# A two-layer attention and retention trunk: the second layer's value projections in couples, and its last output projections joined in one tail

## The chip, the cores and the metric

The kernel runs on one core of a Trainium2 chip. The metric is the device time of one execution in microseconds. The engines are TensorE (PE in the profile; PEld is its weight load), VectorE (DVE), ScalarE (ACT), GpSimd (POOL) and SyncE (SP, which here issues DMAs). L316 and the like are lines of the kernel.

## The reference

512 tokens of width 1024 pass two layers, and a last RMS norm closes them. Layer 0 mixes with causal forgetting attention (12 heads of 128), layer 1 with retention (12 heads, keys of 64, values of 128); both also have 4 heads of cross-attention to 256 memory rows. Each layer is

```python
h = rmsnorm(x, norm_g[i])
q, k, v, ..., q_mem, z = split_cols(h @ w_in, sizes)
o = concat([main(q, k, v), memo(q_mem)], axis=-1) * silu(z)
x = x + o @ w_out[i]
```

In layer 1, `main` is retention: rotary q and k, scores times a decay table, their product with v, and an RMS norm per head. The output is `rmsnorm(x, final_norm_g)`.

## The kernel before

**Split products.** Every matrix product is made of three matmuls on 32-bit parts: a value is cast to a high part H by ScalarE, VectorE subtracts it from the value to make a low part L, and the product is HH + HL + LH. A weight piece of 128x1024 therefore costs a load (raw), an ACT cast (wH, L130) and a DVE subtraction (wL, L131). There are 4 buffers for each of wH and wL and 3 for raw; a piece is prepared when an older one is retired (`retire`, `prep_piece`).

**Layout.** The tokens are 4 blocks of 128 rows. The normed activations h stand transposed as hH and hL. q, k, the memory queries and the gates z are projected feature-major (`f_T`, L209: 24 matmuls of 512 columns in two parts; `f_z` is the gate, `f_rot` adds the rotary step). Heads are worked in pairs: pair p has heads 2p and 2p+1.

**Rotation.** `f_rot` copies the accumulator out (ACT, L243), sends it through four DMAs that swap 32-row groups (SP, L246), multiplies by sine and cosine and adds (DVE, L248 to L250), and splits the sum into the qk tiles (ACT and DVE, L254 to L262; for k the last step is L256). The scores of the pair (`g_ret`, L610) read the qk tiles.

**Values.** `f_v` (L266) makes the values of one pair: 24 matmuls with 256 moving columns for each token block, from two weight pieces. `f_v2` (L299) makes those of two neighbouring pairs: 24 matmuls of 512 columns per block in two parts of 12, from four pieces; it yields eight parts, two per block. Layer 1 uses `f_v` for pairs 0 and 5 and `f_v2` for (1,2) and (3,4).

**Output.** `f_out` multiplies finished gated heads by the output weights for one pair or for two pairs at a time, and adds to x (L336). `f_out_last` makes the very last output projection: it opens three accumulators with the terms that do not need the last gated head, lets that head finish, and closes them.

**Order.** The program is a list of cycles. Each cycle has fillers (parts of projections, in a list) and jobs (steps of the attention or retention generators), and `emit` places a job step after the filler at which it is due; steps not yet due are carried into the next cycle. Tensor matmuls run in exactly this written order. DVE, ACT and POOL are ordered by a scheduler that goes by due times, so the order of their instructions changes when the lists change, but it is fixed in the program. The first cycle of a layer is called its lead, and norm steps of layer 1 (L186 to L196, four token blocks) are carried into the lead. The cycles of layer 1 after the memory heads are numbered by pair, 0 to 5; cycle p computes pair p's heads while its fillers make q and k (`nq`) of pair p+1, the gates `z0` and `z1` of pair p, values, and an output projection.

**End.** `after1` is called on each finished output block of the last layer and makes the final norm: sum of squares (ACT, L813), scale (POOL, L814 and L819), product with the norm weights (DVE, L816), scaling (L821 to L824) and the output DMAs.

Of the kernel before, what the change touches and what calls it, by code (L numbers as in the profile page):

```python
# [36 lines left out]
def tile_hybrid(ctx, tc, x_in, mem_in, memT_in, g_cols, norm_g, fin_g, b_f, wv0, wp, index, consts, cosT, sinT, dec, out):  # L37
# [320 lines left out]
    def f_out_last(l, pr, after, fine=False):  # L358
        keys = [(l, "o", pr, hf) for hf in range(2)]
# [3 lines left out]
        heads = (pr * 2, pr * 2 + 1)  # L363
        opened = {}

        def terms(t, c0, c1):
            o = c0 // 512
            return out_terms(l, pieces[keys[o]], heads, t, c0 - o * 512, c1 - o * 512)

        def begin(blk):  # L370
            ps = acc_tile()[:, :blk[2] - blk[1]]
            for i, (a, b) in enumerate(terms(*blk)[:3]):
                PE.matmul(ps, lhsT=a, rhs=b, start=(i == 0), stop=False)  # L373
            opened[blk] = ps

        def finish(blk):
            ps = opened.pop(blk)
            for i, (a, b) in enumerate(terms(*blk)[3:]):
                PE.matmul(ps, lhsT=a, rhs=b, start=False, stop=(i == 2))  # L379
# [3 lines left out]
        def fn(t):  # L383
            if t == 0:
                for b in blocks[:3]:
# [213 lines left out]
    def g_ret(l, h):  # L599
# [52 lines left out]
        st[l, "g", h] = split_new("gg", sz)  # L652
# [100 lines left out]
    def build_layer(l):  # L753
        M = "fox" if l == 0 else "ret"
# [4 lines left out]
        cycle(f_v(l, 0) + qm[0] + qm[1], start=("lead", l))  # L759
# [5 lines left out]
        v2 = {pr: f_v2(l, (pr, pr + 1)) for pr in (1, 3)}  # L765
        for pr in range(6):
            f = v2[pr][4:] if pr in v2 else []
            z0, z1 = f_z(l, pr * 2), f_z(l, pr * 2 + 1)
            nq = fq(pr + 1) if pr < 5 else []
            if pr == 0:  # L770
                f = f + z0 + z1 + nq[:-2] + f_out(l, (6, 7)) + nq[-2:] + v2[1][:4]
            elif pr in (2, 4):
                o = f_out(l, (pr - 2, pr - 1))
                if pr == 2:
                    f = f + z0 + z1 + nq[:-2] + o + nq[-2:] + v2[3][:4]
                else:
                    f = f + z0 + z1 + nq[:4] + o[:4] + nq[4:] + o[4:]
            elif pr == 5:
                f = f_v(l, 5) + z0 + z1 + f_out(l, (4,))
            elif l == 0:  # L780
                f = f + z0 + z1 + nq
            else:
                f = f + nq + z0 + z1
# [15 lines left out]
    cycle(f_out_last(0, 5, lambda *a: None), [("norm", (t, ("g", 1)), t + 0.5) for t in range(NT)],  # L799
# [5 lines left out]
    def after1(t, c0, c1):  # L805
        src = xt[t][:, c0:c1]
# [3 lines left out]
        ss = small.tile([P, 1], F32, name="ss")  # L810
        r = small.tile([P, 1], F32, name="rstdf", bufs=6)
        junk = tile_("dd", [P, 512])
        A.activation(junk[:, :c1 - c0], src, AF.Square, accum_out=ss)  # L813
        G.tensor_scalar(out=r, in0=ss, scalar1=1.0 / D, scalar2=fin.get((t, "r"), EPS), op0=ALU.mult, op1=ALU.add)  # L814
        fin[t, "r"] = r
        V.tensor_tensor(out=y[:, c0:c1], in0=src, in1=st["g", 2][:, c0:c1], op=ALU.mult)  # L816
        if c1 == D:
            r2 = small.tile([P, 1], F32, name="rstd2")
            G.tensor_tensor(out=r2, in0=r, in1=nhalf, op=ALU.pow)  # L819
            if t >= 1:  # L820
                V.tensor_scalar(out=y[:, :512], in0=y[:, :512], scalar1=r2, scalar2=None, op0=ALU.mult)  # L821
            else:
                A.activation(y[:, :512], y[:, :512], AF.Copy, scale=r2)
            A.activation(y[:, 512:], y[:, 512:], AF.Copy, scale=r2)  # L824
            nc.sync.dma_start(out=out[t * P:(t + 1) * P, :512], in_=y[:, :512])
            A.dma_start(out=out[t * P:(t + 1) * P, 512:], in_=y[:, 512:])

    cycle(f_out_last(1, 5, after1, fine=False), start="end")
# [8 lines left out]
    def emit():  # L837
# [14 lines left out]
        for ci, (fillers, jobs, start, mode, last) in enumerate(cycles):  # L852
# [9 lines left out]
            elif start == "end":  # L862
                st["g", 2] = load_g(fin_g)
            elif start == ("lead", 1):
# [138 lines left out]
```

## Time and profile before

| what | value |
|---|---|
| median of 3 runs | 932.09 us (931.97 to 932.2) |
| the profiled execution | 931.98 us, of it 930.2 us span |
| busy, share of the span | PE 98%, PEld 84%, DVE 64%, ACT 47%, POOL 4% |
| mean granted clock of TensorE | 0.996 |
| mean DMA rate | 108 GB/s |

The span runs from the first to the last recorded instruction; 1.78 us of the time lie outside it. A busy share is a mean over stages. PE is over 90% busy in 38 of the 40 equal slices of the span, all but the first and the last.

### The profile page before, as it was taken

To read this page: it belongs to the slowest core of one execution; us is meant where nothing else is said; L and a number is where in the kernel's file an instruction comes from. 1 tells how busy PE (TensorE), PEld (TensorE's weight loads), DVE (VectorE), ACT (ScalarE), POOL (GpSimd) and SP (SyncE) were. 2 spreads that over 40 slices of the span, in tenths; PEclk is the share of its full clock that TensorE was granted. 3 is DMA by queue.
4 is the path that set the end of the run, shared out by engine and by line. 5 is a ranking of instruction groups with operands and counts; after the bars stand their busy time and mean duration, and the time that the engine had idled before them with its cause. 6 is when DMAs were issued, how large, how long until landed. Compare 5 with 4: busy or idle time off the path is not lost.

```text
span 930.2 us, 12316 instructions
## 1 busy us (share of the span) xinstructions
PE 915.7 (98%) x4611; PEld 777.1 (84%) x4611; DVE 598.3 (64%) x1067; ACT 441.7 (47%) x773; POOL 34.4 (4%) x92
## 2 busy tenths in 40 slices
PE   8999999999999999999999999999999999999995
PEld 6988888888888888888898898888888888888984
DVE  5766664553655564646557756566769676878776
ACT  6654443422544233433325434544557554766464
POOL 0200100000000000000000010000000000000002
PEclk9999999999999999999999999999999999999998
DMA  8963332222322231423232152323324331532302
GB/s 299 337 212 110 111 110 81 90 80 68 125 90 92 72 99 51 139 83 102 80 99 94 46 159 77 105 75 100 98 99 127 93 103 55 159 103 79 115 23 91
DMA packets 32483, 100.69 MB, mean 108 GB/s; under 512 B 4380, under 2 KB 4636, under 8 KB 32424
## 3 DMA queue, kind: packets, MB, share of 16 engines
q1 hardware_dynamic: 30840, 96.76, 32.1%
q0 software_dynamic: 864, 2.10, 0.8%
q10 hardware_dynamic: 720, 1.05, 0.3%
q8 instruction: 36, 0.59, 0.3%
q14 instruction: 23, 0.19, 0.1%
HBM read 92.53 MB, written 4.22 MB: 104 GB/s over the span
## 4 chain that ended last, share of the span: by engine, by line
PE 93%; ACT 2%; DMA 1%; DVE 1%; POOL 1%; issue 1%; POOLq 0%; SPq 0%; ACTq 0%; DVEq 0%
PE acc L220 45%; PE acc L60 21%; PE acc L316 9%; PE s L60 6%; PE o L538 5%; PE acc L434 1%; PE pt L572 1%; PE o L60 1%; DMA x<-in_x_dram 1%; PE pt L507 1%; PE acc L379 1%; PE acc L373 1%; PE pt L196 1%; ACT dd L813 0%; ACT wH L130 0%
## 5 line engine op out<-in xcount | busy, mean ns | idle before, releaser
L131 DVE TENSOR_TENSOR wL<-raw,wH 128x1024 fp32r<-128x1024 f32 x148 | 180.8, 1224 | 99.1 <-ACT wH L130 61.6
L130 ACT CAST wH<-raw 128x1024 fp32r<-128x1024 f32 x148 | 154.6, 1049 | 64.0 <-PE acc L220 31.6
L220 PE MATMUL acc<-hL,wH 128*128 128x512 f32 x608 | 163.5, 395 | 0.0
L220 PE MATMUL acc<-hH,wH 128*128 128x512 f32 x608 | 153.5, 395 | 0.0
L220 PE MATMUL acc<-hH,wL 128*128 128x512 f32 x608 | 150.6, 390 | 0.0
L60 PE MATMUL acc<-wH,gg 128*128 128x512 f32 x448 | 146.6, 393 | 0.0
L220 PEld LDWEIGHTS acc<-hH,wL 128*128 128x128 f32 x608 | 114.2, 188 | 24.4
L220 PEld LDWEIGHTS acc<-hH,wH 128*128 128x128 f32 x608 | 111.2, 188 | 21.2
L220 PEld LDWEIGHTS acc<-hL,wH 128*128 128x128 f32 x608 | 111.2, 188 | 20.6
L60 PEld LDWEIGHTS acc<-wH,gg 128*128 128x128 f32 x448 | 84.2, 188 | 16.8
L60 PE MATMUL acc<-wL,gg 128*128 128x512 f32 x224 | 87.4, 390 | 0.0
L336 DVE TENSOR_TENSOR x<-acc,x 128x512 f32<-128x512 f32 x80 | 54.7, 687 | 36.5 <-PE acc L60 34.5
L151 ACT CAST pTH<-pt 128x128 fp32r<-128x128 f32 (+2 forms) x64 | 29.7, 467 | 63.3 <-PE pt L572 50.6
L562 ACT ACTIVATE p<-dd,nm 128x128 f32<-128x128 f32 (+3 forms) x48 | 27.0, 563 | 67.1 <-DVE nm L558 66.9
L60 PE MATMUL s<-qk 128*128 128x256 f32 (+3 forms) x240 | 53.7, 326 | 0.0
L151 ACT CAST gg<-sz 128x512 fp32r<-128x512 f32 x32 | 19.9, 621 | 64.8 <-DVE sz L473 39.9
L316 PE MATMUL acc<-wH,hH 128*128 128x512 f32 x128 | 50.4, 394 | 0.0
L316 PE MATMUL acc<-wH,hL 128*128 128x512 f32 x128 | 50.0, 390 | 0.0
L316 PE MATMUL acc<-wL,hH 128*128 128x512 f32 x128 | 49.9, 390 | 0.0
L152 DVE TENSOR_TENSOR pTL<-pt,pTH 128x128 fp32r<-128x128 f32 (+2 forms) x64 | 34.3, 537 | 24.3 <-ACT pTH L151 24.1
L60 PEld LDWEIGHTS acc<-wL,gg 128*128 128x128 f32 x224 | 42.2, 188 | 7.7
L538 PE MATMUL o<-pTH,vv 128*128 128x512 f32 (+1 forms) x192 | 48.4, 315 | 0.0
(165 smaller groups left out, 1329.3 us busy)
## 6 DMA issues: line engine op xcount, KB each, us to landing
raw<-in_wp_dram SPq DMA_DIRECT2D x146, 512.0 KB, 3.6
cbc<-c_d SPq DMA_DIRECT2D x12, 256.0 KB, 3.2
cbc<-in_dec_dram SPq DMA_DIRECT2D x12, 256.0 KB, 3.3
dd<-dd SPq DMA_DIRECT2D x48, 64.0 KB, 2.0
x<-in_x_dram SPq DMA_DIRECT2D x4, 512.0 KB, 8.0
raw<-in_wv_dram SPq DMA_DIRECT2D x2, 536.0 KB, 4.2
vv<-in_memT_dram SPq DMA_DIRECT2D x2, 512.0 KB, 4.5
vv<-in_mem_dram SPq DMA_DIRECT2D x2, 512.0 KB, 7.7
```

The lines of the kernel that those rows point to most:

```text
L60: PE.matmul(ps, lhsT=l, rhs=r, start=(i == 0), stop=(i == n - 1))
L130: A.copy(out=H[:, :n], in_=raw[:, :n])
L131: V.tensor_tensor(out=L[:, :n], in0=raw[:, :n], in1=H[:, :n].bitcast(F32), op=ALU.subtract)
L151: A.copy(out=dH, in_=src)
L152: V.tensor_tensor(out=dL, in0=src, in1=dH.bitcast(F32), op=ALU.subtract)
L196: PE.transpose(pt[:, k, :], xn[:, c:c + P], ident)
L220: PE.matmul(box["ps"], lhsT=a[:, k * P:(k + 1) * P], rhs=b[:, k, :], start=(n == 0), stop=(n == 23))
L316: PE.matmul(ps, lhsT=a, rhs=b, start=(k == 0 and n == 0), stop=(k == KD - 1 and n == 2))
L336: V.tensor_tensor(out=dst, in0=ps, in1=dst, op=ALU.add)
L373: PE.matmul(ps, lhsT=a, rhs=b, start=(i == 0), stop=False)
L538: PE.matmul(o[:, j * P:], lhsT=a, rhs=b, start=(j == 0 and i == 0), stop=(j == NT - 1 and i == 2))
L562: A.activation(p[:, :n], dd[:, :n], AF.Exp, bias=nm, scale=-1.0, accum_out=sm)
```

## The change

All value projections of layer 1 are made by `f_v2`, for (0,1), (2,3) and (4,5); the first stands in the lead, the halves of the others at the ends of cycles 1 and 3 and the starts of cycles 2 and 4. The lists of the cycles of layer 1 are rearranged; the output projection of pairs 2 and 3 moves from cycle 4 to cycle 5, between the two gates. The output projections of pairs 4 and 5 are joined in `f_out_last`, which now opens three accumulators with 9 matmuls each instead of 3, and makes the last block in two pieces of 256 columns. The gated heads of pairs 4 and 5 stand in buffers of other tags. The final norm is written in a new way: whole rows are scaled by one DVE instruction, the last block's sum of squares is made on DVE, and DVE, ACT and POOL keep the written order there. Layer 0 keeps its order.

```diff
-    def f_out_last(l, pr, after, fine=False):
-        keys = [(l, "o", pr, hf) for hf in range(2)]
+    def f_out_last(l, prs, after, fine=False):
+        keys = [(l, "o", pr, hf) for hf in range(2) for pr in prs]
         blocks = [(t, c, c + 512) for t in range(NT) for c in (0, 512)]
         if fine:
             blocks[-1:] = [(NT - 1, 512, 768), (NT - 1, 768, 1024)]
-        heads = (pr * 2, pr * 2 + 1)
         opened = {}
+        early = 6 * len(prs) - 3
...
-            return out_terms(l, pieces[keys[o]], heads, t, c0 - o * 512, c1 - o * 512)
+            return sum([out_terms(l, pieces[l, "o", pr, o], (pr * 2, pr * 2 + 1), t, c0 - o * 512, c1 - o * 512) for pr in prs], [])
...
-            for i, (a, b) in enumerate(terms(*blk)[:3]):
+            for i, (a, b) in enumerate(terms(*blk)[:early]):
...
-                for b in blocks[:3]:
+                for b in ((blocks[0], blocks[2], blocks[1]) if len(prs) > 1 else blocks[:3]):
...
-        st[l, "g", h] = split_new("gg", sz)
+        st[l, "g", h] = split_new({4: "km", 5: "qk"}.get(pr, "gg"), sz)
...
-        cycle(f_v(l, 0) + qm[0] + qm[1], start=("lead", l))
+        v2 = {pr: f_v2(l, (pr, pr + 1)) for pr in ((1, 3) if l == 0 else (0, 2, 4))}
+        cycle((f_v(l, 0) if l == 0 else v2[0]) + qm[0] + qm[1], start=("lead", l))
...
-        v2 = {pr: f_v2(l, (pr, pr + 1)) for pr in (1, 3)}
         for pr in range(6):
-            f = v2[pr][4:] if pr in v2 else []
             z0, z1 = f_z(l, pr * 2), f_z(l, pr * 2 + 1)
             nq = fq(pr + 1) if pr < 5 else []
-            if pr == 0:
-                f = f + z0 + z1 + nq[:-2] + f_out(l, (6, 7)) + nq[-2:] + v2[1][:4]
-            elif pr in (2, 4):
-                o = f_out(l, (pr - 2, pr - 1))
-                if pr == 2:
-                    f = f + z0 + z1 + nq[:-2] + o + nq[-2:] + v2[3][:4]
+            o = f_out(l, {0: (6, 7), 2: (0, 1), 4: (2, 3)}[pr]) if pr in (0, 2, 4) else []
+            if l == 0:
+                if pr == 4:
+                    f = z0 + z1 + nq[:4] + o[:4] + nq[4:] + o[4:]
+                elif pr == 5:
+                    f = f_v(l, 5) + z0 + z1 + f_out(l, (4,))
                 else:
-                    f = f + z0 + z1 + nq[:4] + o[:4] + nq[4:] + o[4:]
-            elif pr == 5:
-                f = f_v(l, 5) + z0 + z1 + f_out(l, (4,))
-            elif l == 0:
-                f = f + z0 + z1 + nq
+                    f = (v2[pr][4:] if pr else []) + z0 + z1 + nq if pr % 2 else z0 + z1 + nq[:-2] + o + nq[-2:] + v2[pr + 1][:4]
+            elif pr == 0:
+                f = z0 + z1 + nq + o
+            elif pr in (1, 3):
+                f = nq + z0 + z1 + v2[pr + 1][:4]
+            elif pr == 2:
+                f = v2[2][4:] + z0 + z1 + nq + o
+            elif pr == 4:
+                f, late = v2[4][4:] + z0 + z1 + nq, o
             else:
-                f = f + nq + z0 + z1
+                f = z0 + late + z1
...
+        if last and c0 > 0:
+            r = one("rstdf")
+            prev = fin[t, "r"]
+            V.tensor_tensor_reduce(out=junk, in0=src, in1=src, scale=1.0 / D, scalar=prev, op0=ALU.mult, op1=ALU.add, accum_out=r)
+            fin[t, "r"] = r
+            if c1 < D:
+                return
+            r2 = one("rstd2")
+            G.tensor_tensor(out=r2, in0=r, in1=nhalf, op=ALU.pow)
+            for c in (512, 768):
+                V.scalar_tensor_tensor(out=y[:, c:c + 256], in0=xt[t][:, c:c + 256], scalar=r2, in1=g[:, c:c + 256],
+                                       op0=ALU.mult, op1=ALU.mult)
+                nc.sync.dma_start(out=out[rows, c:c + 256], in_=y[:, c:c + 256])
+            A.activation(y[:, :512], y[:, :512], AF.Copy, scale=r2)
+            A.dma_start(out=out[rows, :512], in_=y[:, :512])
+            return
+        ss = one("ss")
+        A.activation(junk, src, AF.Square, scale=1.0 / 32, accum_out=ss)
+        if "pend" in fin:
+            fin.pop("pend")()
+        r = one("rstdf")
+        G.tensor_tensor(out=r, in0=ss, in1=fin[t, "r"] if c0 else eps_t, op=ALU.add)
+        if last:
+            V.tensor_tensor(out=y[:, :512], in0=src, in1=g[:, :512], op=ALU.mult)
+        if c0 == 0:
+            return
+        r2 = one("rstd2")
+        G.tensor_tensor(out=r2, in0=r, in1=nhalf, op=ALU.pow)
+
+        def scale():
+            V.scalar_tensor_tensor(out=y, in0=xt[t], scalar=r2, in1=g, op0=ALU.mult, op1=ALU.mult)
+            nc.sync.dma_start(out=out[rows, :], in_=y)
+        fin["pend"] = scale
+
+    cycle(f_out_last(1, (4, 5), after1, fine=True), start="end")
...
+                end.enter_context(tc.manual_schedule(engines={mybir.EngineType.DVE, mybir.EngineType.Pool, mybir.EngineType.Activation}))
...
-                ev.append([nF + 1.2, flush_retired])
+                ev.append([nF + 0.2, flush_retired])
```

The first place is the seam of cycles 4 and 5 on PE. `acc_7870` (after) is the key projection of pair 5, `o_7883` the product of head 9 with its values, `acc_7938` the gate of head 10, and `s_7955` the first score of head 10, which reads the rotated keys `qk_7912`. After:

```order
L220 MATMUL acc_7870<-hL_87,wH_7666 128x512 x4
L220 MATMUL acc_7870<-hH_86,wL_7667 128x512 x8
L538 MATMUL o_7883<-pTH_7752,vv_7458 128x256
L538 MATMUL o_7883<-pTL_7753,vv_7458 128x256
L538 MATMUL o_7883<-pTH_7752,vv_7459 128x256
L538 MATMUL o_7883<-pTH_7752,vv_7458 128x128
L538 MATMUL o_7883<-pTL_7753,vv_7458 128x128
L538 MATMUL o_7883<-pTH_7752,vv_7459 128x128
L220 MATMUL acc_7938<-hH_86,wH_7717 128x512 x8
L220 MATMUL acc_7938<-hL_87,wH_7717 128x512 x4
L60 MATMUL s_7955<-qk_7852,qk_7912 128x512
L60 MATMUL s_7955<-qk_7854,qk_7912 128x512
```

Before, the same key projection is `acc_7782`, its rotated keys are `qk_7831`, and what comes behind it is:

```order
L220 MATMUL acc_7782<-hL_87,wH_7588 128x512 x4
L220 MATMUL acc_7782<-hH_86,wL_7589 128x512 x8
L60 MATMUL acc_7843<-wH_7647,gg_7083 128x512
L60 MATMUL acc_7843<-wL_7648,gg_7083 128x512
L60 MATMUL acc_7843<-wH_7647,gg_7084 128x512
L60 MATMUL acc_7843<-wH_7647,gg_7348 128x512
L60 MATMUL acc_7843<-wL_7648,gg_7348 128x512
L60 MATMUL acc_7843<-wH_7647,gg_7349 128x512
L60 MATMUL acc_7843<-wH_7703,gg_7562 128x512
L60 MATMUL acc_7843<-wL_7704,gg_7562 128x512
L60 MATMUL acc_7843<-wH_7703,gg_7563 128x512
```

Before, seven more blocks of that output projection, the steps of heads 8 and 9 and the first value part of pair 5 follow, and only then the score `s_8077<-qk_7757,qk_7831`. After, 6 products with the values and 12 matmuls of a gate stand between the key projection and the score.

The second place is DVE at the same seam, after. `wL_7919` is a weight piece's low part, `dd_7842` the rotation of q of pair 5, `dd_7902` that of k, `km_5068` and `km_5066` are the sine and cosine tables, `km_7820` a part of gated head 8:

```order
L152 TENSOR_TENSOR km_7820<-sz_7714,km_7819 128x512
L248 TENSOR_TENSOR dd_7843<-dd_7843,km_5068 128x512
L249 TENSOR_TENSOR dd_7842<-dd_7842,km_5066 128x512
L131 TENSOR_TENSOR wL_7919<-raw_7721,wH_7918 128x1024
L250 TENSOR_TENSOR dd_7842<-dd_7842,dd_7843 128x512
L633 TENSOR_TENSOR p_7930<-p_7930,dd_7932 64x512
L261 TENSOR_TENSOR qk_7854<-dd_7842,qk_7852 64x512
L648 SCALAR_TENSOR_TENSOR sz_7780<-o_7883,sz_7780 128x512
L635 TENSOR_TENSOR sqs_7931<-p_7930,sqs_7931 64x512
L261 TENSOR_TENSOR qk_7860<-dd_7842,qk_7858 64x512
L248 TENSOR_TENSOR dd_7903<-dd_7903,km_5068 128x512
L249 TENSOR_TENSOR dd_7902<-dd_7902,km_5066 128x512
L250 TENSOR_TENSOR dd_7902<-dd_7902,dd_7903 128x512
L256 TENSOR_TENSOR qk_7912<-dd_7902,qk_7912 64x512
```

The rotation of k (`dd_7902`, `dd_7903`) stands behind the last steps of the rotation of q, behind the weight piece, and behind steps of heads 8 and 9 (`sz_7714`, `p_7930`, `sz_7780`).

The third place is the lead of layer 1 on DVE. `hL` are low parts of the transposed activations, `vv_5050` the last token block's normed rows, `raw_4823` and `raw_4874` the third and fourth weight pieces. Before:

```order
L131 TENSOR_TENSOR wL_5138<-raw_4823,wH_5137 128x1024
L189 SCALAR_TENSOR_TENSOR vv_5050<-x3_85,rstd2_5053,vv_4932 128x1024
L152 TENSOR_TENSOR hL_87<-pt_5097,hH_86 128x4x128
L152 TENSOR_TENSOR hL_87<-pt_5104,hH_86 128x4x128
L131 TENSOR_TENSOR wL_5144<-raw_4874,wH_5143 128x1024
L152 TENSOR_TENSOR vv_5071<-acc_5072,vv_5070 128x512
```

After:

```order
L131 TENSOR_TENSOR wL_5088<-raw_4823,wH_5087 128x1024
L189 SCALAR_TENSOR_TENSOR vv_5050<-x3_85,rstd2_5053,vv_4932 128x1024
L131 TENSOR_TENSOR wL_5094<-raw_4874,wH_5093 128x1024
L152 TENSOR_TENSOR hL_87<-pt_5099,hH_86 128x4x128
L152 TENSOR_TENSOR hL_87<-pt_5106,hH_86 128x4x128
L152 TENSOR_TENSOR vv_5071<-acc_5074,vv_5070 128x256
```

Before, the fourth piece comes behind the activations; after, ahead of them. On PE the third and fourth pieces are read after by the second part of the lead's first token block:

```order
L316 MATMUL acc_5074<-wH_4926,hL_87 128x512
L196 MATMUL pt_5099<-csb_75,vv_5012 128x128 x4
L196 MATMUL pt_5106<-csb_75,vv_5012 128x128 x4
L316 MATMUL acc_5074<-wH_5087,hH_86 128x512
L316 MATMUL acc_5074<-wL_5088,hH_86 128x512
L316 MATMUL acc_5074<-wH_5087,hL_87 128x512
L316 MATMUL acc_5074<-wH_5087,hH_86 128x512
L316 MATMUL acc_5074<-wL_5088,hH_86 128x512
L316 MATMUL acc_5074<-wH_5087,hL_87 128x512
L316 MATMUL acc_5074<-wH_5093,hH_86 128x512
L316 MATMUL acc_5074<-wL_5094,hH_86 128x512
```

Before, the lead's first two blocks read only the first two pieces (`wH_4870` and `wH_4926`), and the third and fourth are first read after four blocks of values.

## Rows read from the trace of the kernel before

**Rows 1.** The profile's page: busy time, share and instructions of each engine.

```profile
PE 915.7 (98%) x4611; PEld 777.1 (84%) x4611; DVE 598.3 (64%) x1067; ACT 441.7 (47%) x773; POOL 34.4 (4%) x92
```

**Rows 2.** Waits of PE, whole program: total us, times, longest us.

```profile
PE acc L434 <- DVE wL L131: 1.6, 2, 0.9
PE acc L845 <- DVE dd L842: 1.4, 1, 1.4
PE acc L434 <- ACT wH L130: 1.4, 1, 1.4
PE pt L177 <- POOL mr L171: 0.4, 1, 0.4
PE acc L379 <- ACT gg L151: 0.3, 1, 0.3
```

**Rows 3.** Chain of waits: start us, us, what.

```profile
535.51 0.87 PE pt L196 x8
...
670.48 2.76 PE acc L316 x12
...
874.77 2.88 PE acc L60 x24
```

**Rows 4.** Timeline, start of layer 1: start us, us, engine line op out<-in xcount.

```profile
535.30 1.21 DVE L131 TENSOR_TENSOR wL<-raw,wH 128x1024 fp32r<-128x1024 f32 x1
...
537.23 1.28 DVE L189 SCALAR_TENSOR_TENSOR vv<-x,rstd,vv 128x1024 f32<-128x1024 f32 x1 [0.72 <-POOL rstd L188]
...
539.63 1.21 DVE L131 TENSOR_TENSOR wL<-raw,wH 128x1024 fp32r<-128x1024 f32 x1
```

**Rows 5.** Timeline, from a key projection's end to its rotated keys (pair 3).

```profile
764.95 0.59 ACT L243 COPY dd<-acc 128x512 f32<-128x512 f32 x1 [0.76 <-PE acc L220]
...
765.57 2.41 SPq L246 DMA_DIRECT2D dd<-dd  x4
...
769.52 0.69 DVE L248 TENSOR_TENSOR dd<-dd,km 128x512 f32<-128x512 f32 x1 [3.29 <-DMA dd<-dd]
...
773.75 1.40 DVE L256 TENSOR_TENSOR qk<-dd,qk 64x512 fp32r<-64x512 f32 x2 [0.35 <-ACT qk L254]
```

**Rows 6.** Timeline, last key projection (pair 5), its rotated keys, first score reading them.

```profile
840.71 2.00 PE L220 MATMUL acc<-hH,wL 128*128 128x512 f32 x8
...
856.36 0.68 DVE L256 TENSOR_TENSOR qk<-dd,qk 64x512 fp32r<-64x512 f32 x1
...
870.68 0.98 PE L60 MATMUL s<-qk 128*128 128x512 f32 x4
```

**Rows 7.** Timeline, end of the program.

```profile
920.47 0.39 PE L379 MATMUL acc<-wH,gg 128*128 128x512 f32 x1
...
923.27 0.68 DVE L336 TENSOR_TENSOR x<-acc,x 128x512 f32<-128x512 f32 x1
...
925.23 0.55 POOL L819 TENSOR_TENSOR rstd<-rstdf,nhalf 128x1 f32<-128x1 f32 x1
...
925.82 0.72 ACT L824 ACTIVATE vv<-vv,rstd 128x512 f32<-128x512 f32 x1 [1.10 <-POOL rstd L819]
```

**Rows 8.** Groups by form: busy us, mean ns | idle before us <-releasers.

```profile
L235 ACT ACT_TABLE_LOAD x6 | 7.7, 1283 | 1.6 <-DVE gg L152 1.5
...
L236 DVE SCALAR_TENSOR_TENSOR sz<-sz,acc 128x512 f32<-128x512 f32 x32 | 21.7, 680 | 5.0 <-ACT sz L235 5.0
...
L151 ACT CAST gg<-sz 128x512 fp32r<-128x512 f32 x32 | 19.9, 621 | 64.8 <-DVE sz L473 39.9 <-PE acc L60 15.2 <-DVE sz L649 6.4
...
L152 DVE TENSOR_TENSOR vv<-acc,vv 128x256 fp32r<-128x256 f32 x36 | 15.1, 419 | 26.6 <-ACT vv L151 26.5
```

**Rows 9.** Timeline of PE, the warm-up at the program's start.

```profile
1.44 4.86 PE L845 MATMUL acc<-dd 128*128 128x512 f32 x13 [1.44 <-DVE dd L842]
```

**Rows 10.** Windows at the end: busy us by engine, granted clock, DMA share, GB/s.

```profile
920.80:923.00 2.20, 0.06 (x1) 0.00 (x0) 2.00 (x5) 1.05 (x4) 0.86 (x2) 1.00 0.62 238
923.00:924.00 1.00, 0.00 (x0) 0.00 (x0) 0.96 (x3) 0.61 (x3) 0.19 (x1) 0.54 0.38 141
```

More of the change, by code (lines that the diff above doesn't have):

```diff
@@ L377, in finish @@
             ps = opened.pop(blk)
-            for i, (a, b) in enumerate(terms(*blk)[3:]):
+            for i, (a, b) in enumerate(terms(*blk)[early:]):
                 PE.matmul(ps, lhsT=a, rhs=b, start=False, stop=(i == 2))
@@ L753, in build_layer @@
     def build_layer(l):
+        late = []
         M = "fox" if l == 0 else "ret"
@@ L797, in tile_hybrid @@
     build_layer(0)
-    cycle(f_out_last(0, 5, lambda *a: None), [("norm", (t, ("g", 1)), t + 0.5) for t in range(NT)],
+    cycle(f_out_last(0, (5,), lambda *a: None), [("norm", (t, ("g", 1)), t + 0.5) for t in range(NT)],
           start="l1", mode=4)
@@ L805, in after1 @@
     def after1(t, c0, c1):
-        src = xt[t][:, c0:c1]
+        last = t == NT - 1
+        rows = slice(t * P, (t + 1) * P)
+        src, g = xt[t][:, c0:c1], st["g", 2]
         if c0 == 0:
@@ L809, in after1 @@
         y = fin[t]
[L810 to L814, printed above, removed]
-        fin[t, "r"] = r
[L816 to L826, printed above, removed]
@@ L828, in tile_hybrid, with one @@
-    cycle(f_out_last(1, 5, after1, fine=False), start="end")
+        def one(name):
+            return small.tile([P, 1], F32, name=name, bufs=4)
+        junk = tile_("dd", [P, 512])[:, :c1 - c0]
+        if last and c0 > 0:
[14 more added lines that the diff above has]
+            return
@@ L899, in emit @@
                 carry = [[p - nF, f] for p, f in ev]
+    end = ExitStack()
     tri = cst.tile([P, P], F32R, name="tri")
@@ L907, in tile_hybrid @@
         emit()
+        end.close()
 def _tcols(w, c):
@@ L959 @@
                 continue
-            if pr in (1, 3):
+            if pr in ((1, 3) if l == 0 else (0, 2, 4)):
                 for i, a in enumerate(_vcols(w, [(v0 + pr * 256, v0 + pr * 256 + 512)], 2)):
                     add(a, l, "v2", pr, i)
-            elif pr in (0, 5):
+            elif l == 0 and pr in (0, 5):
                 for i, a in enumerate(_vcols(w, [(v0 + pr * 256, v0 + pr * 256 + 256)], 4)):
```

## The prediction

> **What bounds the kernel now.** I read the page's busy times first: PE is busy 98% of the span, DVE 64%, ACT 47% [rows 1]. Then I read PE's waits for the whole program [rows 2]. There are only five groups, 5.1 us together. The groups on L434, L845 and L177 belong to the start of the program, and the last, 0.3 us, is the gate of head 11 ahead of the last output projection. The reader is to see what is not there: no wait for rotated keys, values, weight pieces or layer 1's norm. From the warm start on PE is a queue that never runs dry, so a matmul saved there is saved in full, and a wait added there is paid in full. Third, the timeline of the end: the last matmul starts at 920.47 and lasts 0.39, and the span ends at 930.2 [rows 7], so 9.3 us follow in which PE has no work. The sum therefore has two kinds of terms: PE's queue, and the 9.3 us behind it. It is made against the profiled execution, 931.98 us (span 930.2, 1.78 outside it), 0.1 under the median of 932.09.
>
> **The change, part by part.**
>
> *Value projections.* Pairs 0 and 5 were eight blocks of 24 matmuls with 256 columns, 2.88 us each on the chain; a part of 12 with 512 columns takes 2.76 [rows 3]. The same work becomes eight such parts: 8 x (2.76 - 2.88) = -0.96. The couples that were there already only change their place and partner.
> The Trainium skill, TensorE: Matmul & The Clock Gate, "Back-to-back issue gap", gives a gap of N/2.4 + 2.5 ns; by that 12 of 512 against 24 of 256 would be a saving of 30 ns a part, 0.24 in all. The rows, 0.12 a part, decide.
>
> *Last block in two pieces.* Twelve matmuls of 512 columns become 24 of 256: by the same two rows +0.12.
>
> *Gate of head 11.* 27 matmuls instead of 9 now stand ahead of its use: 27 x 0.23 (2.76/12, [rows 3]) = 6.2 us of cover. What they cover has grown too: before, the projection of pair 4 lay between the last gate's projection and the tail; now the tail comes at once. From the gate's projection on: a table load (1.28), tanh (near 0.6), four DVE steps (0.68 each) and a cast (0.62) [rows 8], 5.2, and with the handoffs and a weight cast ahead on ACT 6 to 7. The wait stays near the 0.3 of [rows 2] or the 0.9 that the whole gate now costs with its low part: I take 0, ends -0.5 and +1.
>
> *The end.* Before, DVE's backlog put the last add at 923.27, 2.4 after the last matmul's end; POOL's power ran at 925.23 (0.55) and the last scale at 925.82 (0.72); 3.66 followed to the span's end for the output DMA [rows 7]. After, the last piece has 256 columns: an add and a custom sum of squares (0.42 each, the nearest row is the 256-column subtraction of [rows 8]), the power 0.55, a scale of 0.72, and some 0.4 of handoffs: 2.5, then 3.7 for the same DMA. 6.2 instead of 9.3 is -3.1. The custom sum's form doesn't stand in the trace; if it took 512 columns' time (0.68) and the backlog stayed by half, -1.9; without any handoff -3.6.
>
> *The lead of layer 1.* Before, the first blocks read two weight pieces; now the second part of the first block reads the third and the fourth. They can't come earlier: they take buffers that the output projection of layer 0's pair 5 gives back. The third is ready on DVE at 535.30 + 1.21 = 536.5, PE comes to it at 536.3 (the eight transposes end at 535.51 + 0.87 = 536.38 [rows 3], less 0.12): 0.25 of wait. The fourth stands behind the norm of the last token block, which waits for POOL and runs 537.23 to 538.51 [rows 4]; with 1.21 for itself it is ready at 539.7, and PE wants it at about 538.0, six matmuls (1.4) after the third. 0.25 + 1.75 = +2.0. Ends: 0.3 (the norm comes earlier and hides it) and 3.7 (twice the wait for the norm).
>
> *The seam of cycles 4 and 5.* This is the term that decides. Before, the key projection of pair 5 ends at 842.71, its first rotated keys are there at 857.04, and the first score that reads them starts at 870.68, 28 us after the projection [rows 6]; the wait was hidden under a whole output projection. After, in written order, only six short products (some 0.5) and 12 matmuls of 512 columns (2.76) lie between: 3.2 us of cover. The chain itself is not shortened. For pair 3 the copy starts at 764.95, the swapped rows are there at 769.52, the first rotated keys at 773.75 + 0.70 = 774.45: 9.5 us, the fastest of the pairs with a short way [rows 5]; back to back it would be 4.57 + three DVE steps of 0.69 + a cast of 0.62 + 0.70 = 8.0. After, q's rotation stands ahead of k's on DVE and ACT, and a weight subtraction stands ahead of q's last step whose buffer PE frees only with the key projection's last matmul. Walking that from the key projection's end: weight 1.2, q's L250 0.7, then five casts on ACT (0.62 each) with one step of a head between (0.6) and a DVE step (0.69) while k's DMAs land at 4.6; k's three DVE steps come behind q's last, at 6.3 to 8.4, then a cast 0.62, L256 0.69, and 0.5 of handoffs: 10.2. PE waits 10.2 - 3.2 = +7.0. Ends: 8.0 - 3.2 = 4.8, and by pair 5's own 14.33 [rows 6] 11.1. Behind the waiting score on PE stand all of cycle 5's matmuls, so nothing fills it.
>
> *Clock.* PE idles 7 us there. At the end of the program, where PE is idle from 920.86 on, the granted clock was 1.00 over 920.8 to 923.0 and 0.54 in the next microsecond [rows 10]: the higher of its two levels of 2.4 and 1.2 GHz, and then nearly the lower. I take it that it falls in the 7 us too, and not in the lead, whose waits are shorter and have matmuls between them. What the climb back costs the trace shows at the start: 13 matmuls in 4.86 us [rows 9] against 13 x 0.23 + 0.17 = 3.2 at the pace of [rows 3]: +1.7, ends 0 (it doesn't fall) and 1.7.
> The Trainium skill, the same page, "Why this matters for your kernels", warns of idle gaps of TensorE between bursts, since the clock drops in them: by it 938.7 stands, and without it the sum would be 937.0. This trace agrees at its end and has no such gap in the middle of the work.
>
> Sum: -0.96 + 0.12 + 0 - 3.1 + 2.0 + 7.0 + 1.7 = +6.8; 931.98 + 6.8 = 938.7 us.
>
> **The rivals.**
>
> *Longer wait at the seam.* Couples of values for pairs 2 to 5 put more splits into cycles 3 and 4, and DVE may be behind when it comes to the rotation. For it: pair 5's chain took 14.33 in a full cycle. Against: DVE is 64% busy over the span [rows 1], and its order there is fixed. It would give a wait of 11: 938.7 + 4.1 = 942.8.
>
> *Short waits.* The rotation runs back to back (4.8), the lead costs 0.3, the clock does not fall: -3.9 + 0.3 + 4.8 = +1.2, or 933.2, within 0.2% (1.9 us, about what a measurement of this kernel can tell from no change). For it: at the seam DVE has no work it need not do. Against: the order fixes q ahead of k.
>
> *Both waits are covered; faster.* The terms without waits are -0.96 + 0.12 - 3.1 = -3.9, 928.0 us. The mechanism is at the seam alone: if the score of head 10 finds its keys ready, because the tail of cycle 4 is late on PE anyway for another reason (an accumulator not yet read, carried head steps) and the way to the score is long in time if short in matmuls. It decides when seam and lead together cost under 2 us. For it: the order of PE shows matmuls, not times. Against: 3.2 us of cover against the back-to-back 8.0, a gap that no row closes.
>
> *The change doesn't do what it says:* if 512 columns were not faster in the couples, the -0.96 would fall away, 939.7; this lies in the forecast's own range.
>
> **How the numbers follow.** Forecast (seam near 7, clock once): 0.67, its own range 935.5 to 941.5. Longer wait: 0.13. Short waits: 0.10. Covered: 0.10. Slower by over 0.2% are the forecast, the longer wait and the upper edge of the short case: 0.81; same 0.09; faster 0.10. The range 932.8 to 943.0 leaves out the covered case, part of the short one, and the upper half of the longest waits' tail, under 2 in 10.
>
> **What the profile after would show.** PE's waits should have a new row, s <- DVE qk (L256), one time, near 7 us, and one or two rows of acc <- DVE wL in the lead, near 2 together. PE's stream around it should show one gap, with DVE and ACT going through q's rotation and then k's inside it, and the first matmuls behind it at the slower pace. The chain's L60 pieces of 24 should be gone from layer 1. From the last matmul to the span's end there should be some 6.2 us. The forecast is wrong if the new row is missing or under 3 us, if the lead shows no wait, or if the end keeps its 9 us.

## The result and the profile after

The changed kernel takes 940.77 us (median of 4 runs, 939.65 to 941.8) against 932.07: ratio 1.009, interval 1.0078 to 1.0103. It is slower by 8.7 us. In a later set of runs it took 941.76 against 932.47, 9.3 more. The profiled execution, the fastest of the four, took 939.65, 7.67 more than the one of before, with a span of 937.8.

The waits of PE in the changed kernel (total us, times, longest us), to be held against [rows 2]:

```profile
PE s L60 <- DVE qk L256: 5.9, 1, 5.9
PE acc L434 <- DVE wL L131: 1.5, 2, 0.8
PE acc L316 <- DVE wL L131: 1.5, 1, 1.5
PE acc L872 <- DVE dd L869: 1.4, 1, 1.4
PE acc L434 <- ACT wH L130: 0.9, 1, 0.9
PE s L60 <- DVE p L612: 0.8, 1, 0.8
PE s L60 <- DVE sqs L635: 0.2, 1, 0.2
```

Three groups are new in the middle of the program: the rotated keys (L256), a weight piece in the lead (L316 for wL L131), and scores that wait for L612 and L635. The wait for head 11's gate is gone.

The seam of cycles 4 and 5, from the timeline of the changed kernel, in the order of the chain: the cover on PE, then copy, DMAs, the weight subtraction, the last step of q's rotation, the first and the last of k's, the waiting score, and the matmuls behind it. It answers to [rows 5, 6].

```profile
862.69 1.08 PE L220 MATMUL acc<-hL,wH 128*128 128x512 f32 x4
...
860.35 0.59 ACT L243 COPY dd<-acc 128x512 f32<-128x512 f32 x1 [0.77 <-PE acc L220]
...
860.96 2.41 SPq L246 DMA_DIRECT2D dd<-dd  x4
...
860.41 1.22 DVE L131 TENSOR_TENSOR wL<-raw,wH 128x1024 fp32r<-128x1024 f32 x1 [0.46 <-issue]
...
865.48 0.69 DVE L261 TENSOR_TENSOR qk<-dd,qk 64x512 fp32r<-64x512 f32 x1 [0.55 <-ACT qk L254]
...
866.20 0.69 DVE L248 TENSOR_TENSOR dd<-dd,km 128x512 f32<-128x512 f32 x1
...
868.90 1.41 DVE L256 TENSOR_TENSOR qk<-dd,qk 64x512 fp32r<-64x512 f32 x2 [0.68 <-ACT qk L254]
...
869.65 1.86 PE L60 MATMUL s<-qk 128*128 128x512 f32 x4 [5.88 <-DVE qk L256]
...
871.30 1.80 PE L220 MATMUL acc<-hL,wH 128*128 128x512 f32 x4
```

The key projection ends at 860.3 (the copy starts at 860.35). The cover runs out at 863.60: four matmuls from 862.69 on at 0.23. The k steps start at 866.20, right behind q's last at 865.48, though the four DMA issues had ended at 860.96 + 2.41 = 863.37. The first keys are there at 868.90 + 0.70 = 869.60, and the score starts at 869.65: 6.05 us of idle PE. Four matmuls of 512 columns then take 1.80, against 1.08 for the four at 862.69.

Windows of the changed kernel around this gap (us; PE, PEld, DVE, ACT, POOL busy; granted clock, DMA share, GB/s), to be held against [rows 10]:

```profile
863.60:865.60 2.00, 0.17 (x1) 0.00 (x0) 1.42 (x4) 1.94 (x4) 0.00 (x0) 1.00 0.67 145
865.60:867.60 2.00, 0.00 (x0) 0.00 (x0) 1.93 (x4) 1.10 (x2) 0.00 (x0) 0.61 0.39 156
867.60:869.60 2.00, 0.00 (x0) 0.00 (x0) 1.30 (x2) 1.23 (x2) 0.00 (x0) 0.50 0.00 0
869.60:873.00 3.40, 3.35 (x9) 2.83 (x10) 2.55 (x5) 1.03 (x2) 0.00 (x0) 0.52 0.00 0
873.00:876.00 3.00, 3.00 (x16) 2.52 (x15) 1.46 (x3) 2.05 (x2) 0.00 (x0) 1.00 0.02 5
```

The clock is granted in full (2.4 GHz) for the first 2 us of the gap, falls in the next, is at half (1.2 GHz) when the score comes, and is back at 873 in this execution.

The lead of layer 1, DVE and PE, and on the chain the couple's matmuls behind it; it answers to [rows 3, 4]:

```profile
536.02 1.22 DVE L131 TENSOR_TENSOR wL<-raw,wH 128x1024 fp32r<-128x1024 f32 x1
...
537.95 1.28 DVE L189 SCALAR_TENSOR_TENSOR vv<-x,rstd,vv 128x1024 f32<-128x1024 f32 x1 [0.72 <-POOL rstd L188]
...
539.15 1.22 DVE L131 TENSOR_TENSOR wL<-raw,wH 128x1024 fp32r<-128x1024 f32 x1
...
540.43 0.50 PE L316 MATMUL acc<-wL,hH 128*128 128x512 f32 x1 [1.51 <-DVE wL L131]
...
542.73 16.34 PE acc L316 x72
```

The third piece's low part (536.02) is followed by the norm of the last token block (537.95) and only then by the fourth piece's (539.15 to 540.37), for which PE waits until 540.43. The 72 matmuls of the next six parts take 16.34, 2.72 a part, against 2.88 for 24 of 256 columns [rows 3].

The end of the changed kernel, to be held against [rows 7]:

```profile
930.71 0.28 PE L379 MATMUL acc<-wH,qk 128*128 128x256 f32 x1
...
931.53 0.42 DVE L336 TENSOR_TENSOR x<-acc,x 128x256 f32<-128x256 f32 x1
...
932.10 0.48 DVE L823 CUSTOM_DVE_ANT_0 dd<-x,rstdf 128x256 f32<-128x256 f32 x1
...
932.67 0.55 POOL L828 TENSOR_TENSOR rstd<-rstdf,nhalf 128x1 f32<-128x1 f32 x1 [2.58 <-DVE rstdf L823]
...
933.25 0.72 ACT L833 ACTIVATE vv<-vv,rstd 128x512 f32<-128x512 f32 x1 [3.58 <-POOL rstd L828]
```

The last matmul ends at 930.99 and the span at 937.8: 6.8 us, where it was 9.3.

### The profile page after: what moved, and what is told of

It reads as the page before. It is cut to its first block, busy times and chain, and to the rows that moved or that the text cites. A ratio compares the mean times of both kernels' runs of the same rounds, so it can differ in the third digit from the quotient of the medians.

```text
span 937.8 us, 12153 instructions
## 1 busy us (share of the span) xinstructions
PE 918.6 (98%) x4527; PEld 774.8 (83%) x4527; DVE 594.6 (63%) x1063; ACT 441.7 (47%) x772; POOL 34.5 (4%) x91
## 4 chain that ended last, share of the span: by engine, by line
PE 92%; DVE 3%; ACT 3%; issue 1%; DMA 1%; POOL 1%; POOLq 0%; SPq 0%; DVEq 0%; ACTq 0%
PE acc L220 42%; PE acc L60 19%; PE acc L316 11%; PE s L60 5%; PE o L538 4%; PE acc L434 3%; PE acc L373 2%; PE pt L572 1%; PE o L60 1%; PE acc L379 1%; DVE wL L131 1%; PE pt L507 1%; ACT wH L130 1%; DMA vv<-in_memT_dram 0%; PE pt L196 0%
## 5 line engine op out<-in xcount | busy, mean ns | idle before, releaser
L131 DVE TENSOR_TENSOR wL<-raw,wH 128x1024 fp32r<-128x1024 f32 x148 | 180.9, 1224 | 102.5 <-ACT wH L130 60.2
L60 PE MATMUL acc<-wH,gg 128*128 128x512 f32 x416 | 136.0, 393 | 0.0
L60 PEld LDWEIGHTS acc<-wH,gg 128*128 128x128 f32 x416 | 78.1, 188 | 15.5
L60 PE MATMUL acc<-wL,gg 128*128 128x512 f32 x208 | 81.1, 390 | 0.0
L336 DVE TENSOR_TENSOR x<-acc,x 128x512 f32<-128x512 f32 (+1 forms) x73 | 49.6, 681 | 37.6 <-PE acc L60 30.6
L316 PE MATMUL acc<-wL,hH 128*128 128x512 f32 x160 | 62.6, 391 | 1.6 <-DVE wL L131 1.5
L316 PE MATMUL acc<-wH,hH 128*128 128x512 f32 x160 | 63.1, 394 | 0.0
L316 PE MATMUL acc<-wH,hL 128*128 128x512 f32 x160 | 62.4, 390 | 0.0
L60 PEld LDWEIGHTS s<-qk 128*128 128x128 f32 x240 | 40.8, 191 | 14.0 <-DVE qk L256 6.3
L152 DVE TENSOR_TENSOR vv<-acc,vv 128x256 fp32r<-128x256 f32 (+1 forms) x46 | 19.9, 432 | 44.5 <-ACT vv L151 44.5
```

The costliest lines, as they stand in the source:

```text
L60: PE.matmul(ps, lhsT=l, rhs=r, start=(i == 0), stop=(i == n - 1))
L131: V.tensor_tensor(out=L[:, :n], in0=raw[:, :n], in1=H[:, :n].bitcast(F32), op=ALU.subtract)
L152: V.tensor_tensor(out=dL, in0=src, in1=dH.bitcast(F32), op=ALU.subtract)
L316: PE.matmul(ps, lhsT=a, rhs=b, start=(k == 0 and n == 0), stop=(k == KD - 1 and n == 2))
L336: V.tensor_tensor(out=dst, in0=ps, in1=dst, op=ALU.add)
```

## The experiments

Differences are taken against the kernel before in the same set of runs. The edits are against the changed kernel unless said.

**Later scores in cycle 5.**

```diff
-                base = 4 if pr == 0 else 0
+                base = {0: 4, 5: 6}.get(pr, 0)
...
-                      mode=SPAN5 if pr == 5 else 14 + base, last=pr == 5)
+                      mode=SPAN5 + base if pr == 5 else 14 + base, last=pr == 5)
```

> The changed kernel with one edit: the steps of heads 10 and 11 start 6 units later in cycle 5, so that some 24 gate matmuls, 24 of the output projection and the 6 short products (11 to 12 us on TensorE) lie between pair 5's key projection and the first score. Theory (the seam wait and the clock behind it are the loss): the row s <- DVE qk L256 (5.9 us, one time) goes, the 1.6 us of slow pace behind it goes, the time falls by 7.5 from the changed kernel's median of 940.8 to 933.3 (932.7 to 934). Rival 1 (VectorE is behind in cycles 3 to 5, the wait only shows there): a new wait of 3 us or more stands at a later score or output block, time 936 or more. Rival 2 (the loss is in the lead and the rest): time stays over 939.

Measured: 935.43 against 932.6 (ratio 1.0031, 1.002 to 1.0042), +2.8. So 5.9 of the 8.7 are gone, not the 7.5 that were expected, and the time lies above the expected 932.7 to 934; the slow matmuls are gone. Two rows of PE's waits tell where part of the rest stayed:

```profile
PE s L60 <- DVE qk L256: 0.8, 1, 0.8
...
PE s L60 <- DVE p L612: 1.6, 3, 0.8
```

The keys are still late by 0.8, at 11.7 us of cover (counted from the copy of the key projection), and scores wait for L612 three times where it was once. The theory holds for most of it; the chain to the keys has become longer with the cover. That was tested by itself below.

**A busy seam.** A part of 26 matmuls (`lhsT=hH[:, 0, :P], rhs=hH[:, 0, :]`) into an accumulator nobody reads:

```diff
-                f = z0 + late + z1
+                f = [(z0[0][0], lambda: (z0[0][1](), warm_gap()))] + z0[1:] + late + z1
```

> The changed kernel with 26 extra matmuls of 512 columns (26 x 0.23 = 5.9 us), whose result nobody reads, set between the gate's first part and the first score of head 10. They fill the wait with work and change nothing else. Theory (the wait is for the rotated keys, and the idle time lowers the clock, which costs a further 1.6 us): the wait on L256 falls under 0.4 us, the granted clock stays 1.00 through the seam, no slow matmuls behind it; time 940.8 - 1.6 = 939.2 (938.7 to 939.7). Rival 1 (the slow matmuls behind the gap have another cause): time stays at 940.8 or more. Rival 2 (what is waited for is not the rotation, but follows the matmuls): +5.9, 946.7. If the clock's change is also what spreads the times (939.65 to 941.8 for the changed kernel, 931.97 to 932.2 for the one before), the spread is under 0.5 us here.

Measured: 938.87 against 932.6 (1.0065, 1.0053 to 1.0078), +6.3. PE now:

```profile
863.44 6.05 PE L757 MATMUL acc<-hH 128*128 128x512 f32 x26
...
869.49 1.09 PE L61 MATMUL s<-qk 128*128 128x512 f32 x4
```

The score starts at 869.49, as the last of them ends, where it started 6.05 behind the gate. It has no wait row, and four matmuls take 1.09 where they took 1.86. The granted clock is 1.00 throughout. PE did 6 us of useless work in the same place and the time fell, from 8.7 over the kernel before (9.3 in the later set) to 6.3: idling has a price of its own beside the wait.

That price is not the same in every execution. The 16 matmuls of 512 columns from the first score on take 3.69 here (869.49 to 873.18) and 5.11 in the first profile of the changed kernel (869.65 to 874.76), 1.4 more. In the second profile of the changed kernel, the same 16 end where the next score starts:

```profile
870.18 1.86 PE L60 MATMUL s<-qk 128*128 128x512 f32 x4 [5.87 <-DVE qk L256]
...
876.30 0.39 PE L60 MATMUL s<-qk 128*128 128x256 f32 x2
```

That is 6.12, 2.4 more. In the other three profiles below that keep this gap (lead from two pieces, one piece, gate first) they take 6.48, 6.18 and 5.65. So the price lies between 1.4 and 2.8, and the 2.4 of the times is among these.

The expected spread under 0.5 us did not come (937.87 to 939.11). The kernel before, which has no such gap, spread by 1.1 in these runs too, so this gap is not the only source. That the clock is not behind the spread can't be said: of the 19 executions of the kernel before that stand beside the tail alone, the ten with a mean granted clock of 0.994 to 0.996 took 932.37 to 933.18, the nine with 0.997 or 0.998 took 931.8 to 932.47.

**The lead from two pieces.**

```diff
-        cycle((f_v(l, 0) if l == 0 else v2[0]) + qm[0] + qm[1], start=("lead", l))
+        cycle((f_v(l, 0) if l == 0 else f_v(l, 0) + f_v(l, 1)) + qm[0] + qm[1], start=("lead", l))
```

(and the weight pieces of pairs 0 and 1 laid out for it).

> The changed kernel with the values of pairs 0 and 1 in the lead made in blocks of 24 matmuls with 256 columns, from two weight pieces at a time, as before, in place of the couple; all else as changed. Theory (the lead's 2.0 us are a wait for the third and fourth weight pieces' low parts): the row acc L316 <- DVE wL goes, 8 x 0.12 = 1.0 us of matmul time comes back: 940.8 - 1.0 = 939.8 (939.3 to 940.3). Rival (the lead waits for the norm of the token blocks, whatever reads the pieces): the wait stays near 2 and the matmuls cost 1.0 more: 941.8.

Measured: 940.81 against 932.6 (1.0091, 1.0077 to 1.0105), +8.2, which can't be told from the changed kernel's 8.7 to 9.3. In the trace the wait row of L316 is gone, so the theory of the wait holds; that the lead's 2.0 us come back in the time is not shown. They are used up elsewhere in this profile: 8 blocks of 256 columns at 2.88 in place of 2.72 cost 1.3, waits of scores are 0.5 longer (1.0 for L612 where it was 0.8, 0.5 for L635 where it was 0.2), and the slow matmuls behind the seam cost 2.8 where they cost 1.4 in the first profile of the changed kernel.

**The last block in one piece.** `fine=False` in the last `f_out_last`.

> The changed kernel with the last output block in one piece of 512 columns in place of two of 256. Theory: little. The last add (0.69) and custom sum (0.7) take 0.5 us more after the last matmul, but they no longer stand behind the sum of the piece before (which held up the last add by 0.4), and TensorE gains 0.12: the end from the last matmul is 6.7 to 7.0 against 6.8, the time within 0.3 of 940.8. Rival (the split pays, as it is the last column count that sets the end): +0.5 or more.

Measured: 941.04 against 932.6 (1.0091, 1.0077 to 1.0105), +8.4: no difference. Its add, custom sum and power:

```profile
933.16 0.69 DVE L336 TENSOR_TENSOR x<-acc,x 128x512 f32<-128x512 f32 x1 [0.23 <-PE acc L379]
...
934.00 0.75 DVE L823 CUSTOM_DVE_ANT_0 dd<-x,rstdf 128x512 f32<-128x512 f32 x1
...
934.83 0.55 POOL L828 TENSOR_TENSOR rstd<-rstdf,nhalf 128x1 f32<-128x1 f32 x1 [2.46 <-DVE rstdf L823]
```

From the last matmul's end (933.12) to the span's end (940.0) it is 6.9, against 6.8 with two pieces, where the last add stood behind the sum of the piece before. No gain of the split is seen.

**The tail alone**, on the kernel before:

```diff
-    cycle(f_out_last(1, 5, after1, fine=False), start="end")
+    cycle(f_out_last(1, (4, 5), after1, fine=True), start="end")
...
-                    f = f + z0 + z1 + nq[:4] + o[:4] + nq[4:] + o[4:]
+                    f = f + z0 + z1 + nq[:4] + o[:4] + nq[4:] + (o[4:] if l == 0 else [])
+                    late = o[4:]
             elif pr == 5:
-                f = f_v(l, 5) + z0 + z1 + f_out(l, (4,))
+                f = f_v(l, 5) + z0 + z1 + (f_out(l, (4,)) if l == 0 else late)
```

with the changed `f_out_last`, gate tags and `after1`, the written order at the end, and `nF + 0.2` in place of `nF + 1.2` (the last line of the change).

> The kernel before with the change's tail alone: output projections of pairs 4 and 5 joined behind head 11's gate, the last block in two pieces, the new final norm in written order. The value projections and the lists of cycles 0 to 3 stay as before; half of the output projection of pairs 2 and 3 moves from cycle 4 to cycle 5, where the one of pair 4 was. Theory (the tail is a gain and the lists are the loss): the end falls from 9.3 to 6.8 (-2.5), the wait for head 11's gate goes (-0.9), the split costs 0.12, no new wait of TensorE: -3.3 against the kernel before in the same runs. Rival (joining needs the lists to be squeezed: cycle 4 has 12 fillers for the steps it had 16 for, and the waits come with it): waits of 3 us or more in cycles 4 and 5, no gain.

Measured: 928.87 (928.52 to 928.95) against 932.47, ratio 0.996 (0.9947 to 0.9974): -3.6. It beats both kernels. All of PE's waits:

```profile
PE acc L434 <- DVE wL L131: 1.5, 2, 0.8
PE acc L434 <- ACT wH L130: 1.5, 1, 1.5
PE acc L869 <- DVE dd L866: 1.4, 1, 1.4
PE pt L177 <- POOL mr L171: 0.4, 1, 0.4
```

Nothing stands there behind the start of the program; the last matmul ends 6.8 before the span does. The tail is the gain, as expected; what stands ahead of it in the change, the couples and the lists of cycles together, is the loss.

**The new norm behind one pair's output projection**, on the kernel before: the same, with `f_out_last(1, (5,), after1, fine=True)`, `f_out(l, (4,))` in cycle 5 and the old tags.

> The kernel before with only the new final norm, the last block in two pieces and the written order of the three engines at the end; the last output projection is pair 5's alone, as before, and all lists are as before. Theory: the end falls by 2.5 and the rest stays: -2.4 against the kernel before in the same runs, head 11's gate still waited for. Rival (it is the joining, 12 instead of 6 matmuls per block, that lets VectorE keep up with the blocks, not the way the norm is written): the end stays over 8 us and the gain is under 1.

Measured: 934.59 against 932.47 (1.0024, 1.0015 to 1.0033), +2.1, where -2.4 was expected. The theory falls and the rival holds, by more than it said: the last matmul ends at 922.94, and 9.9 us follow. DVE and PE near the end:

```profile
920.03 1.28 DVE L847 SCALAR_TENSOR_TENSOR vv<-x,rstd,vv 128x1024 f32<-128x1024 f32 x1 [1.24 <-POOL rstd L844]
...
921.23 1.28 DVE L336 TENSOR_TENSOR x<-acc,x 128x512 f32<-128x512 f32 x2
...
921.97 0.38 PE L373 MATMUL acc<-wH,gg 128*128 128x256 f32 x1 [1.35 <-DVE x L336]
```

With one pair a block of 512 columns is 6 matmuls, 1.4 us. In written order the scale of a whole row (1.28) waits for POOL's power ahead of the adds of the next blocks (921.23); PE waits for such an add until 921.97, and DVE is behind to the end. With two pairs a block is 2.7 us of matmuls and DVE is through in time. Without the joining the new norm is a loss. The joining with the old norm was not run, so the share of each in the 3.6 stays open.

**Both places mended**: later scores and the lead from two pieces.

> The changed kernel with both edits of the first runs: scores of heads 10 and 11 six units later, and the values of pairs 0 and 1 in the lead from two pieces with 256 columns. Theory (the two places add): 5.5 from the one, 0.3 to 1.0 from the other, so 1.6 to 2.8 us over the kernel before in the same runs; what is left are small waits of scores on VectorE in cycles 3 to 5 (2 to 3 us). Rival (a wait that is taken away comes back at the next place): no better than with the later scores alone, 2.8 over before or more.

Measured: 934.39 against 932.47 (1.002, 1.0011 to 1.003), +1.9, in the expected range; the profile, of the slowest of its nine executions (936.29), shows no wait in the lead, 0.8 for the keys, and 2.5 of scores that wait for L612 and L635. That the two add fully is not shown: against the later scores alone (+2.8) the intervals overlap. This profile shows something else: two waits of scores in cycle 3, 0.86 before 806.03 and 0.81 before 807.34, are followed by a low clock, with matmuls 0.43 apart (columns as in the windows above: the granted clock is the third number from the end).

```profile
808.00:811.00 3.00, 3.00 (x9) 2.34 (x8) 3.00 (x5) 2.97 (x5) 0.00 (x0) 0.51 0.26 89
```

In the first profile of the changed kernel, with waits of 0.21 and 0.80 at this place, the granted clock is 1.00 over the same 3 us.

**The changed kernel again.**

> The changed kernel once more beside the kernel before, on the chip of this set of runs: 8.2 to 9.2 us over it, with the wait of 5.9 us for the rotated keys, the lead's wait of 1.5 and the slow matmuls behind the first, as in its first profile.

Measured: 941.76 against 932.47 (1.0099, 1.0086 to 1.0113), +9.3, 0.1 above the expected range; the same waits, 5.9 and 1.5.

**Half the cover**: the edit of the later scores with 2 in place of 6 for pair 5.

> The changed kernel with the steps of heads 10 and 11 two units later in cycle 5 instead of six: 24 matmuls of the gate (5.5 us) in place of 12 (2.7) lie before the first score. VectorE's order shifts with it: a weight subtraction (1.2) and a gate step (0.7) now stand ahead of the keys' last step L256. Theory A (the way from the key projection to the keys is fixed, 9.3 us from its copy, and the wait is what is left over): the wait falls by the 2.7 of cover, from 5.9 to 3.2. Theory B (the way is as long as VectorE's queue makes it): the cover gained is mostly given back by the 1.9 us of work put ahead, the wait is 4.5 to 5.5. In either case, if a wait of this size lowers the clock as the longer one did, 1.6 us of slow matmuls follow it; if they don't, the time falls by that too. Times against the changed kernel in the last runs (9.3 over the one before): A with the clock lowered 6.6 over, A without 5.0 over, B with the clock lowered 8.0 to 9.0 over.

Measured: 941.49 against 932.56 (1.0092, 1.0075 to 1.0109), +8.9. DVE ahead of the keys, and the score:

```profile
868.38 1.22 DVE L131 TENSOR_TENSOR wL<-raw,wH 128x1024 fp32r<-128x1024 f32 x1
...
870.72 0.69 DVE L236 SCALAR_TENSOR_TENSOR sz<-sz,acc 128x512 f32<-128x512 f32 x1 [0.51 <-ACT sz L235]
...
871.43 1.40 DVE L256 TENSOR_TENSOR qk<-dd,qk 64x512 fp32r<-64x512 f32 x2
...
872.17 1.22 PE L60 MATMUL s<-qk 128*128 128x512 f32 x2 [4.72 <-DVE qk L256]
```

Theory B holds: 2.7 us of cover brought the wait from 5.9 to 4.7 only, as the weight subtraction and the gate step stand ahead of L256. From the copy of the key projection (861.31) to the first keys it is 10.8 us, where it is 9.2 in the changed kernel; with the later scores it is 12.6. The clock falls in this gap too, and scores behind it wait more often, so nothing is left of the 1.2 us.

**The gate first in cycle 3.**

```diff
-                f = nq + z0 + z1 + v2[pr + 1][:4]
+                f = (nq + z0 if pr == 1 else z0 + nq) + z1 + v2[pr + 1][:4]
```

> The changed kernel with one edit in cycle 3: the gate of head 6 ahead of pair 4's queries and keys, not behind them, so that VectorE has the rotated keys' last steps (L256) behind the first two scores' products (L612) and not between them. Theory (the 1.5 us of waits at 806 to 808, which the forecast did not have, come from those steps standing ahead of L612): the two waits there (s <- DVE sqs 0.2 and s <- DVE p 0.8) go, 1.3 to 1.6 us less than the changed kernel's 9.3 over the kernel before: 7.7 to 8.0 over, the seam's 5.9 unchanged. Rival (VectorE has too much to do in cycle 3 in whatever order): 1 us or more of waits for it stands elsewhere in cycles 3 and 4, time unchanged.

Measured: 939.48 against 932.13 (1.008, 1.0066 to 1.0093), +7.35. That is below the expected 7.7 to 8.0, and 1.35 below the first set's 8.7, but the intervals overlap; the wait rows decide. The waits of scores for L612 and L635 are gone from the whole program, those of the lead and the seam are unchanged. This is what the place looks like in the changed kernel, DVE and then PE:

```profile
804.31 0.69 DVE L256 TENSOR_TENSOR qk<-dd,qk 64x512 fp32r<-64x512 f32 x1
...
805.02 0.69 DVE L612 TENSOR_TENSOR p<-s,cbc 128x512 f32<-128x512 f32 x1
...
806.46 0.69 DVE L256 TENSOR_TENSOR qk<-dd,qk 64x512 fp32r<-64x512 f32 x1
...
807.18 0.56 DVE L612 TENSOR_TENSOR p<-s,cbc 128x384 f32<-128x384 f32 x1
...
807.79 0.50 PE L60 MATMUL s<-qk 128*128 128x256 f32 x2 [0.80 <-DVE p L612]
```

The steps of the rotated keys (804.31, 806.46) stand ahead of the two products of the first scores (805.02, 807.18), and the third score, which needs the second's place in PSUM, waits until 807.79.

## Why the prediction was right, point by point

The direction, the place and the size were right: +6.8 forecast, +7.7 between the profiled executions, +8.7 between the medians. None of the three signs of being wrong came: the new wait row is 5.9, the lead waits, the end is 6.8. By terms, from the first profile after:

| term | forecast | measured | from |
|---|---|---|---|
| value parts and the last block's split | -0.84 | -1.1 | 2.72 a part |
| gate of head 11 | 0 | -1.0 | before, 18 matmuls around it took 908.82 to 913.90 |
| end | -3.1 | -2.5 | 9.3 to 6.8 |
| lead | +2.0 | +2.0 | 0.34 and 1.67 between matmul starts |
| seam | +7.0 | +6.05 | 863.60 to 869.65 |
| clock | +1.7 | +1.4 | 16 starts behind the gap, against 0.23 each |
| scores in cycle 3 | none | +1.5 | 0.37 and 1.08 at 806 to 808 |
| start of the program | none | +0.7 | a matmul at 47.04, now 47.75 |

They sum to 7.05 of the 7.67; the other 0.6 is not found. The experiments show the seam (busy seam, later scores), the clock (busy seam), the end and the gate (tail alone); the lead (two pieces) and cycle 3 (gate first) are shown by the wait rows that go, not by the times. That the sum came so close is partly luck: the forecast was 2.5 too high in values, gate, seam and clock together, and 2.8 too low in end, cycle 3 and start.

The +0.7 of the start is not the change's, since the same instructions stand there. It goes with the granted clock over 9 to 13 us, first in the kernel before, then in the changed one (columns as in the windows above):

```profile
9.00:13.00 4.00, 4.00 (x18) 3.30 (x19) 4.00 (x7) 4.00 (x9) 0.00 (x0) 1.00 1.03 409
...
9.00:13.00 4.00, 4.00 (x11) 3.17 (x12) 4.00 (x7) 4.00 (x9) 0.00 (x0) 0.57 1.04 410
```

Six of the twelve profiles (both of the changed kernel, lead from two pieces, one piece, both places mended, half the cover) have a low clock there, and this matmul at 47.5 to 48.3. In the other six it lies at 46.9 to 47.4, and three of those are variants of the changed kernel (later scores, busy seam, gate first). So some 0.7 us between two single profiles can say nothing of the change.

*The term that failed most* is the gate: I let the longer way to it eat all of the new cover. Its cast is done at 914.1, and PE's 27 early matmuls from 908.92 on last until 915.0.

```profile
913.50 0.62 ACT L151 CAST qk<-sz 128x512 fp32r<-128x512 f32 x1 [2.93 <-DVE sz L651]
```

Before, only 0.3 of the 1.0 stood in the wait row [rows 2]; the rest lay in late starts around it. The end came out 0.6 short of its forecast because the last add stands behind the custom sum of the piece before (931.53, 0.54 after the last matmul), and each piece's handoff is near 0.15.

*The seam* came 1 us shorter than the walk: the walk was right in its order (weight, q, then k) but added 0.5 of handoffs that the rows don't show (k's sum ends at 868.22, its cast starts at 868.25), it lets the k steps start 0.25 too late, and its cover is 0.25 short. The reason it gives is only half the story, though. It took the way to the keys as a fixed length that the old 28 us of distance merely covered. The later-scores and half-cover runs show that the way grows as cover is given, from 9.2 to 12.6, because the order of DVE follows the due times: what was hidden before was hidden by a far larger distance than the chain's length.

*The clock* fell in the gap and not in the lead, as forecast; 1.4 to 2.8 against 1.7 is right in the main. But the term was sized by the program's start, where the granted clock reads 1.00 over 2 to 6 us although 13 matmuls take 4.86 [rows 9]. That this slowness is the clock's climb is not shown, so the nearness is in part luck. The profiled execution had the smallest price of the five profiles with this gap, which fits its being the fastest of its four.

*What was missed* is cycle 3, for which the sum has no term. The wait there is not for keys but for DVE, which the keys' steps keep from the scores. The rival with DVE's load named it for the seam, where it did not decide.

*The rivals.* "Both waits are covered" and "short waits" are out by the wait rows; the longer wait (11) did not come. The couples do what they say: 2.72 a part.

## What to carry to other kernels

Where PE never waits, measure for every producer how many microseconds of PE work lie between it and its reader, and treat a move that shrinks this distance below the chain's length as a cost in full; a rotation through DMAs cost 9 to 13 us here, and its length moved with the cover. A gap of 6 us was paid once more, with 1.4 to 2.8 us, until the clock came back. Look at the clock of single stretches before two profiles are held against each other. Split a change before judging it: the tail alone gave -3.6 us where the whole gave +8.7, and the new norm without the joining gave +2.1.

## What was not expected of the hardware

Useless matmuls shortened the program: 26 of them in the gap of 6 us, at 0.23 each, took 2.4 us off the time (8.7 to 6.3 over the kernel before). Gaps of 6.05 us and of 4.7 us both let the granted clock fall to 0.50 and were each followed by matmuls of 512 columns 0.43 apart. How long it stayed there differed between executions of the same kernel: the 16 matmuls behind the gap took 5.11 in one and 6.12 in the other. Short waits can be followed by a low clock too: 0.57 over 9 to 13 us in one profile and 1.00 in another, at the same instructions, and 0.51 behind two waits of 0.86 and 0.81 us in cycle 3, where waits of 0.21 and 0.80 left it at 1.00.
